# Streaming encoder layer: the prompt's down-projection as seven 2x2 block products, the samples' down-projection beside the up-projection

## The chip, the cores and the metric

The kernel runs on one core of a Trainium2 chip. The metric is the device time in microseconds (us) of one execution. Times are compared as medians of several executions on the same chip; a profiled execution is a further one, of which the hardware profiler recorded every instruction of the five engines (PE, the matrix engine; DVE, the vector engine; ACT, the scalar engine; POOL, the GpSimd engine; SP, which issues the DMAs) and every DMA.

## The reference

One layer of a streaming encoder, for 1024 prompt rows and 8 x 16 = 128 sample rows that share all weights, in float32. The first half (attention, spatial gating, output projection) is not touched by the change. The second half is this:

```python
def conv_ffn(h, conv_cache, w_ffn_in, ffn_conv_w, ffn_conv_b, w_ffn_out):
    g, u = jnp.split(h @ w_ffn_in, 2, axis=-1)          # 1024 -> 2 x 2816
    gp = jnp.concatenate([conv_cache, g], axis=1)
    gc = ffn_conv_b
    for j in range(3):
        gc = gc + ffn_conv_w[j] * gp[:, j:j + T]
    out = (jax.nn.gelu(gc) * u) @ w_ffn_out             # 2816 -> 1024
    return out, gp[:, -2:]
...
x = x + gt2 * conv_ffn(h2, ...)
```

The product with `w_ffn_in` is called the up-projection here, the one with `w_ffn_out` the down-projection. 2816 features are NF = 22 blocks of 128; 1152 rows are 9 tiles of 128 (tile 8 holds the samples).

## The kernel before

**Precision.** Every float32 operand of a matmul is split into a high and a low part (`split`, L77 and L78: ACT copies the high part out, DVE subtracts it from the source), and each product of two operands is three matmuls: high x high, high x low, low x high.

**Up-projection (`unit`, `plain_unit`, `up_weights`).** The kernel already computes it by Winograd's form of Strassen's method: an output of 2x2 blocks from seven block products instead of eight, with sums and differences of blocks on both sides. The operand sums S1 to S4 of the activations stay in SBUF for the whole stage; those of the weights (T1 to T4) are made for every block f of 128 features: four loads into a ring of five staging buffers, four differences on POOL (L1090, L1091, L1095, L1099), seven splits into a ring of nine weight buffers (`wp`). Each f has two units (u = 0, 1; 288 columns of rows each, twice), each of seven products of 12 matmuls 128x288. Unit f = 0, u = 1 is a plain one of eight products. The results go through the convolution (`conv`), GELU and the gate product (`gated`, L1260), and the gated rows are written to DRAM tile by tile (`aT_d[f]`, L1261).

**Order of the work.** Up to the end of f = 0 the order on PE, ACT and DVE is written out by hand (`by_hand`): generators such as `between` (operands of unit pair 0, made during the output projection), `block_pair_1` (operands of unit pair 1, made during f = 0) and `up_weights` are stepped at chosen places of the loops, and an instruction waits behind what stands ahead of it on its engine. From f = 1 on a planner places each instruction by a simulated time: on an engine it takes the ready instruction that is earliest in the program, so instructions whose data and buffers are ready can move ahead. Each engine still runs its own list in order.

**Down-projection (`down_steps`).** It runs at the end. Three groups of three row tiles; in each group, for f = 0..21, a block of `aT_d[f]` (384 rows) and two halves of a row block of `w_ffn_out` are loaded and split, and 3 tiles x 2 halves x 3 matmuls 128x512 are added into six PSUM banks (L1356). The last two f of a group are done tile by tile (`manual_schedule` for PE), and each finished bank is multiplied by the gate (L1389), added to the residual row (L1390) and stored (L1391). The first matmuls of group 0 are stepped during the last unit of the up-projection. `gate_rows` (L824 to L828) issues one load for the prompt's gate and eight for the samples', for each half.

PSUM has six banks of the tag "mm" (X, Y, Z of two units; later the six accumulators) and two of the tag "tp" (transposes). SBUF pools that matter: `xp` (six tiles, operands of the up-projection), `slot` (14 buffers), `wp` (9), `wst` (5 staging buffers).

## Time and profile before

| | |
|---|---|
| median of 3 runs | 1684.75 us (1682.96 to 1686.4) |
| profiled execution, its own time | 1687.31 us |
| its span, first to last instruction | 1685.6 us |
| mean granted TensorE clock | 0.991 |
| up-projection | about 901 to 1417 us of the span |
| down-projection, alone on PE | 1418.6 to 1681 us |

The page gives the busy time of each engine, then the span in 40 slices, the chain of work that ended last, and the costliest groups of instructions. A group's row reads: line, engine, operation, output<-inputs, shape, count | busy time and mean duration of one | idle time of the engine just before them and what ended it. Matmuls overlap each other, so the busy time of a group divided by its count is the pace, and the mean duration is longer than the pace.

### The profile page before, as it was taken

How to read it: one execution, taken by the hardware profiler on the slowest of the kernel's cores; microseconds unless marked ns; L12 is line 12 of the kernel's file. 1: busy time of each engine (PE TensorE's matmuls, PEld its weight loads, DVE VectorE, ACT ScalarE, POOL GpSimd, SP SyncE). 2: the span in 40 equal slices, each digit the busy share in tenths (PEclk: the TensorE clock that was granted, in tenths of full speed). 3: DMA queues.
4: the chain of work that ended last, by engine and by line, in shares of the span. 5: the costliest groups of instructions: out<-in, count | busy, mean ns of one | idle time of the engine just before them, and what ended most of it. 6: DMA issues, size and time to landing. Idle time of an engine off the chain costs nothing.

```text
span 1685.6 us, 28830 instructions
## 1 busy us (share of the span) xinstructions
PE 1642.5 (97%) x10800; PEld 1496.2 (89%) x10800; DVE 926.0 (55%) x1996; ACT 726.0 (43%) x1579; POOL 325.8 (19%) x497
## 2 busy tenths in 40 slices
PE   6999999999999999999997999999999999999998
PEld 4799888799998989999876999999999999888887
DVE  4552111127656643556467877767666675464544
ACT  5443111126655543554245544544444445444342
POOL 5510000015324310024211322222222220000000
PEclk9999999999999999999998999999999999999999
DMA  9215444531110033274532222222222225575765
GB/s 351 72 59 165 150 128 135 175 91 34 50 30 25 22 108 101 88 233 146 178 108 69 84 79 77 68 78 67 70 76 79 80 78 167 181 249 185 229 197 163
DMA packets 166225, 199.15 MB, mean 118 GB/s; under 512 B 14152, under 2 KB 124980, under 8 KB 166085
## 3 DMA queue, kind: packets, MB, share of 16 engines
q1 hardware_dynamic: 166085, 197.31, 36.8%
q8 instruction: 85, 1.39, 0.4%
q14 instruction: 55, 0.45, 0.1%
HBM read 161.74 MB, written 37.57 MB: 118 GB/s over the span
## 4 chain that ended last, share of the span: by engine, by line
PE 90%; DVE 4%; ACT 2%; DMA 2%; issue 1%; SPq 0%; POOL 0%; DVEq 0%; ACTq 0%; POOLq 0%
PE X L1221 16%; PE fops L1356 16%; PE Z L1221 8%; PE Y L1221 4%; PE mxps L1176 4%; PE o L688 2%; PE gbps L103 2%; PE qkps L101 2%; PE gbps L101 2%; PE gbps L102 2%; PE qkps L103 2%; PE qkps L102 2%; PE gaps L101 2%; PE gaps L102 2%; PE gaps L103 2%; PE adaps L382 2%
## 5 line engine op out<-in xcount | busy, mean ns | idle before, releaser
L1356 PE MATMUL fops<-wfo,a 128*128 128x512 f32 x1188 | 270.5, 389 | 0.0
L1356 PEld LDWEIGHTS fops<-wfo,a 128*128 128x128 f32 x1188 | 222.7, 188 | 46.0
L1221 PE MATMUL X<-op,wT 128*128 128x288 f32 x1200 | 190.2, 297 | 6.9 <-ACT u L1283 5.9
L1221 PEld LDWEIGHTS X<-op,wT 128*128 128x128 f32 x1200 | 171.2, 189 | 8.3 <-ACT u L1283 6.4
L1176 PE MATMUL mxps<-wo,mT 128*128 128x512 f32 x432 | 104.6, 397 | 0.5 <-DVE wo L78 0.5
L1176 PEld LDWEIGHTS mxps<-wo,mT 128*128 128x128 f32 x432 | 79.9, 189 | 17.7 <-DVE wo L78 1.1
L1254 DVE SCALAR_TENSOR_TENSOR gc<-gp,parT,gc 128x288 f32<-128x288 f32 (+2 forms) x110 | 65.3, 608 | 42.2 <-ACT gc L1253 42.1
L101 PE MATMUL qkps<-wqk,h1T 128*128 128x256 f32 x288 | 83.5, 290 | 1.0 <-ACT qf L582 1.0
L102 PE MATMUL qkps<-wqk,h1T 128*128 128x256 f32 x288 | 81.9, 284 | 0.0
L103 PE MATMUL qkps<-wqk,h1T 128*128 128x256 f32 x288 | 81.8, 284 | 0.0
L1221 PE MATMUL Z<-opS1h,wT 128*128 128x288 f32 x344 | 76.0, 295 | 0.0
L1253 ACT ACTIVATE gc<-gp,parT 128x288 f32<-128x288 f32 (+2 forms) x110 | 58.9, 573 | 35.3 <-DVE gp L1240 28.8
L1090 POOL TENSOR_TENSOR t<-b,b 128x512 f32<-128x512 f32 x22 | 29.1, 1321 | 224.5 <-DVE wB L78 172.9
L1256 ACT ACTIVATE gc<-gc 128x288 f32<-128x288 f32 x88 | 39.0, 443 | 70.7 <-DVE gc L1255 70.7
L101 PE MATMUL gaps<-h1T,wga 128*128 128x384 f32 x192 | 66.5, 346 | 0.0
L103 PE MATMUL gbps<-h1T,wgb 128*128 128x384 f32 x192 | 65.9, 343 | 0.0
L102 PE MATMUL gaps<-h1T,wga 128*128 128x384 f32 x192 | 65.0, 339 | 0.0
L101 PE MATMUL gbps<-h1T,wgb 128*128 128x384 f32 x192 | 64.9, 338 | 0.0
L102 PE MATMUL gbps<-h1T,wgb 128*128 128x384 f32 x192 | 64.7, 337 | 0.0
L78 DVE TENSOR_TENSOR wB<-b,wB 128x512 fp32r<-128x512 f32 x66 | 57.5, 874 | 12.5 <-ACT wB L77 11.3
L103 PE MATMUL gaps<-h1T,wga 128*128 128x384 f32 x192 | 64.2, 338 | 0.0
L1291 DVE TENSOR_TENSOR upb<-Z,u 128x288 f32<-128x288 f32 x43 | 19.6, 455 | 75.6 <-ACT u L1289 75.6
(497 smaller groups left out, 4339.5 us busy)
## 6 DMA issues: line engine op xcount, KB each, us to landing
adaw<-in_w_ada_dram SPq DMA_DIRECT2D x48, 512.0 KB, 6.5
b<-in_w_ffn_in_dram SPq DMA_DIRECT2D x88, 256.0 KB, 3.1
wfo_0s<-in_w_ffn_out_dram SPq DMA_DIRECT2D x66, 256.0 KB, 3.0
wfo_1s<-in_w_ffn_out_dram SPq DMA_DIRECT2D x66, 256.0 KB, 2.6
aT_d<-gc SPq DMA_DIRECT2D x88, 144.0 KB, 1.8
mb_d<-sgb SPq DMA_DIRECT2D x8, 576.0 KB, 2.7
ga_d<-ga SPq DMA_DIRECT2D x24, 192.0 KB, 1.8
sga<-ga_d SPq DMA_DIRECT2D x8, 576.0 KB, 4.3
```

What stands on the lines that cost most here:

```text
L78: (eng or dve).tensor_tensor(lo, src, hi.bitcast(F32), ALU.subtract)
L101: pe.matmul(ps, lhsT=ah, rhs=bh, start=(i == 0), stop=False)
L102: pe.matmul(ps, lhsT=ah, rhs=bl, start=False, stop=False)
L103: pe.matmul(ps, lhsT=al, rhs=bh, start=False, stop=(i == n - 1))
L382: pe.matmul(ps[32 * j:32 * j + 32, :], lhsT=cT[:, k, :], rhs=st[j // 2][:, (j % 2) * 512:(j % 2 + 1) * 512], start=(k == 0), stop=(k == KD ...
L688: pe.matmul(o[hs, :], lhsT=v[:, k0 // P + i, hs], rhs=out[t, x][:, i * P:(i + 1) * P], start=(i == 0), stop=(i == nk - 1))
L1176: pe.matmul(ps, lhsT=a[:, k, o:o + P], rhs=w[:, b, :], start=(k == n == 0), stop=(k == KD - 1 and n == 2))
L1221: pe.matmul(ps, lhsT=w[:, wj, ks], rhs=x, start=(begin and n == 0), stop=(n == 11), skip_group_check=True)
L1253: act.activation(g, a0, AF.Identity, bias=bb, scale=w0)
L1254: dve.scalar_tensor_tensor(g, a1, w1, g, ALU.mult, ALU.add)
L1256: act.activation(gc, gc, AF.Gelu_apprx_tanh)
L1356: pe.matmul(acc[t, hf], lhsT=a[:, x, o], rhs=w[hf][:, y, :], start=(f == 0 and i == 0), stop=(f == NF - 1 and i == 2))
```

## The change

The down-projection of the eight prompt tiles becomes a 2x2 block scheme: rows 0 to 511 and 512 to 1023, features 0 to 1407 and 1408 to 2815 (NK = 11 blocks each), output columns 0 to 511 and 512 to 1023. Seven products (`KINDS`), each over 11 blocks k and four row tiles at once, three matmuls 128x512 each, replace eight; four PSUM banks X and four Z take the sums. The activation blocks lie whole in SBUF (in the six `xp` tiles and in slots) and S1 to S4 are formed there, S1 on POOL, S2, S3, S4 on DVE, each in place of a block no longer needed. Of the weight sums, T1 is formed in the up-projection and parked in DRAM (`t1_d`), T2 is formed in product S2xT2 and parked (`t2_d`), T3 and T4 are formed in their products, all on POOL with a second operand loaded through three buffers. `prepare` is called three steps ahead of `multiply`; the last four steps are done tile by tile.

The samples' tile leaves the down stage: `gated` splits its 128 columns into `asT[f]`, and `sample_down(f - 1, half)` is called in block f, unit 0, at i = 2 and 3. It loads and splits a half of a row block of `w_ffn_out` (staging and weight rings are shared with `up_weights`) and adds three matmuls into one of the two "tp" banks, which are held until `samples_out`.

In the part ordered by hand, `between` takes its last three splits under the condition that row tile 5 is scaled instead of finished; `block_pair_1` loses one empty step and is stepped once instead of twice at the start; the weights of f = 0 are stepped one place earlier; of the weights of f = 1, four are made in f = 0 (at i = 1, 5, 6, 7) and three in f = 1. The down stage no longer starts inside the last unit, and its loads of gates and cached rows come after its first steps.

```diff
--- before.py
+++ after.py
@@ -135,7 +135,10 @@
     mb_d = dram.tile([KD, P, TOK], F32, name="mb_d")
     ga_d = dram.tile([KD, P, TOK], F32, name="ga_d")
     x1_d = dram.tile([TOK, D], F32, name="x1_d")
-    aT_d = [dram.tile([P, TOK], F32, name=f"aT_d{f}") for f in range(NF)]
+    aT_d = [dram.tile([P, SEQ], F32, name=f"aT_d{f}") for f in range(NF)]
+    NK = NF // 2
+    t1_d = [dram.tile([P, 512], F32, name=f"t1_d{k}") for k in range(NK)]
+    t2_d = [dram.tile([P, 512], F32, name=f"t2_d{k}") for k in range(NK)]
     rel_d = dram.tile([H, 512], F32, name="rel_d")
     relx_d = dram.tile([H, P, 512], F32, name="relx_d")
 
@@ -993,7 +996,7 @@
         o.chunks(1, ("S3h", "S3l", "A22l", "S4h", "S4l"))
         for n in ("S3", "A22", "S4"):
             o.split(n, HOME[n])
-            yield 5, False, 1.3, 1.4
+            yield 5, True, 1.3, 1.4
 
     def block_pair_1():
 
@@ -1033,7 +1036,6 @@
         yield
         o.slots(["S1h"])
         low_slot(o, "S1")
-        yield
         yield
         yield
         o.g["S3h"], o.g["S3l"] = o.g["A21h"], o.g["A21l"]
@@ -1204,7 +1206,8 @@
         step_n += 1
         do_later()
     g1pool.close()
-    fp = ctx.enter_context(tc.tile_pool(name="fp", bufs=1))
+    ffn = ctx.enter_context(ExitStack())
+    fp = ffn.enter_context(tc.tile_pool(name="fp", bufs=1))
 
     def vtile(name, n=QB):
         return fp.tile([P, NV], F32, tag="v", name=name, bufs=16)[:, :n]
@@ -1258,7 +1261,28 @@
 
     def gated(f, c, gc, up):
         dve.tensor_tensor(gc, gc, up, ALU.mult)
-        sp.dma_start(aT_d[f][:, c * QB:(c + 1) * QB], gc)
+        if c == 0:
+            asT[f] = fp.tile([P, 2, P], F32R, tag="as", name=f"as{f}", bufs=2)
+            split(asT[f][:, 0, :], asT[f][:, 1, :], gc[:, :P])
+            gc = gc[:, P:]
+        sp.dma_start(aT_d[f][:, max(c * QB - P, 0):(c + 1) * QB - P], gc)
+    asT, acc_s, raw_s = {}, [], {}
+    def sample_down(f, hf):
+        if f == 0:
+            acc_s.append(tpps(f"sm{hf}"))
+        st = staged(f"ws{f}_{hf}")
+        sp.dma_start(st, wfo[f * P:(f + 1) * P, hf * 512:(hf + 1) * 512])
+        w = wp.tile([P, 2, 512], F32R, tag="w", name=f"wsm{f}_{hf}")
+        split(w[:, 0, :], w[:, 1, :], st)
+        raw_s[hf] = st
+        for i, (x, y) in enumerate(((0, 0), (0, 1), (1, 0))):
+            pe.matmul(acc_s[hf], lhsT=asT[f][:, x, :], rhs=w[:, y, :], start=(f == 0 and i == 0), stop=(f == NF - 1 and i == 2), skip_group_check=True)
+        if hf and f < NK:
+            pool.tensor_tensor(st, st, raw_s[0], ALU.subtract)
+            sp.dma_start(t1_d[f], st)
 
     def unit(f, u, W):
 
@@ -1337,59 +1361,161 @@
             sp.dma_start(cs_[i * P - n0:i * P - n0 + n, :], glo[0:n, i, :])
 
 
-    def down_steps():
...
+    KINDS = [("A11", "B11"), ("A12", "B21"), ("S2", "T2"), ("S1", "T1"), ("S3", "T3"), ("A22", "T4"), ("S4", "B22")]
+    def down():
+        dn = ctx.enter_context(tc.tile_pool(name="dn", bufs=1))
+        g2p, g2s = (dn.tile([P, D], F32, name=n) for n in ("g2p", "g2s"))
+        xs = [xp.tile([P, 3, SEQ], F32, tag=f"x{a}{c}", name=f"ar{c}{a}") for c in range(NC) for a in range(2)]
+        rows = [xs[f // 3][:, f % 3, :] if f < 18 else stile(SEQ, f"ar{f}") for f in range(NF)]
+        s1 = [stile(SEQ, f"ar_s{i}") for i in range((NK + 1) // 2)]
+        kept = {n: [stile(SEQ, f"{n}{i}") for i in range(2)] for n in ("c", "u")}
+        def keep(n, i):
+            return kept[n][i // 2][:, 512 * (i % 2):512 * (i % 2 + 1)]
+        def block(n, k):
+            if n == "S1":
+                return s1[k // 2][:, 512 * (k % 2):512 * (k % 2 + 1)]
+            return rows[k + (NK if n[1] == "2" else 0)][:, 512 * (n[0] == "2"):512 * (n[0] == "2") + 512]
+        def load_a(n, k):
+            f = k + (NK if n[1] == "2" else 0)
+            c = 512 * (n[0] == "2")
+            sp.dma_start(block(n, k), aT_d[f][:, c:c + 512])
+        HOMES = {"A11": "11", "A12": "12", "A22": "22", "S1": "S1", "S2": "11", "S3": "21", "S4": "12"}
+        ops, X, Z = {}, [], []
+        def weight_rows(n, k):
+            f = k + (NK if n[0] == "2" else 0)
+            c = 512 * (n[1] == "2")
+            return wfo[f * P:(f + 1) * P, c:c + 512]
+        def get(src, nm, second=False):
+            t = dn.tile([P, 512], F32, tag="sub", name=nm, bufs=3) if second else staged(nm)
+            sp.dma_start(t, src)
+            return t
+        def prepare(j, k):
+            A, B = KINDS[j]
+            if j == 0:
+                load_a("11", k)
+                load_a("12", k)
+            if j == 1:
+                load_a("21", k)
+                load_a("22", k)
+            if B[0] == "B":
+                t = get(weight_rows(B[1:], k), f"d{B}_{k}")
+            elif B == "T1":
+                t = get(t1_d[k], f"d{B}_{k}")
+            else:
+                x, y = {"T2": (weight_rows("22", k), t1_d[k]), "T3": (weight_rows("22", k), weight_rows("12", k)), "T4": (weight_rows("21", k), t2_d[k])}[B]
+                t, t2 = get(x, f"d{B}_{k}"), get(y, f"d{B}y_{k}", True)
+                pool.tensor_tensor(t, t, t2, ALU.subtract)
+                if B == "T2":
+                    sp.dma_start(t2_d[k], t)
+            w = wp.tile([P, 2, 512], F32R, tag="w", name=f"dw{j}_{k}")
+            split(w[:, 0, :], w[:, 1, :], t)
+            b11, b12, b21, b22, bs1 = (block(n, k) for n in ("11", "12", "21", "22", "S1"))
+            if j == 1:
+                pool.tensor_tensor(bs1, b21, b22, ALU.add)
+            if A == "S2":
+                dve.tensor_tensor(b11, bs1, b11, ALU.subtract)
+            if A == "S3":
+                dve.tensor_tensor(b21, b22, b11, ALU.subtract)
+            if A == "S4":
+                dve.tensor_tensor(b12, b12, b11, ALU.subtract)
+            a = wp.tile([P, 2, 512], F32R, tag="w", name=f"da{j}_{k}")
+            split(a[:, 0, :], a[:, 1, :], block(HOMES[A], k))
+            ops[j, k] = a, w
+        def x1_rows(t, hf):
+            r = dn.tile([P, 512], F32, tag="x1r", name=f"x1r{t}_{hf}", bufs=3)
+            sp.dma_start(r, x1_d[t * P:(t + 1) * P, 512 * hf:512 * (hf + 1)])
+            return r
+        def y_rows(t):
+            return io["o_yp"].rearrange("b s d -> (b s) d")[t * P:(t + 1) * P, :] if t < NTP else io["o_ys"].rearrange("b s d -> (b s) d")
+        def finish(j, i):
+            lo, hi = slice(0, 512), slice(512, 1024)
+            c, u = keep("c", i), keep("u", i)
+            if j == 0:
+                act.activation(c, X[i], AF.Copy)
+            if j == 1:
+                r = x1_rows(i, 0)
+                dve.tensor_tensor(c, Z[i], c, ALU.add)
+                dve.tensor_tensor(c, c, g2p[:, lo], ALU.mult)
+                pool.tensor_tensor(c, c, r, ALU.add)
+                sp.dma_start(y_rows(i)[:, lo], c)
+            if j == 2:
+                r = x1_rows(i, 1)
+                act.activation(u, X[i], AF.Copy)
+                pool.tensor_tensor(u, u, g2p[:, hi], ALU.mult)
+                pool.tensor_tensor(u, u, r, ALU.add)
+            if j == 4:
+                r = x1_rows(i + 4, 1)
+                act.activation(c, X[i], AF.Copy)
+                dve.tensor_tensor(c, Z[i], c, ALU.add)
+                dve.tensor_tensor(c, c, g2p[:, hi], ALU.mult)
+                pool.tensor_tensor(c, c, r, ALU.add)
+                sp.dma_start(y_rows(i + 4)[:, hi], c)
+            if j == 5:
+                r = x1_rows(i + 4, 0)
+                dve.tensor_tensor(c, X[i], g2p[:, lo], ALU.mult)
+                dve.tensor_tensor(c, c, r, ALU.add)
+                sp.dma_start(y_rows(i + 4)[:, lo], c)
+            if j == 6:
+                n = 2 if i == 3 else 1
+                for p in range(n):
+                    a, b = 512 * p // n, 512 * (p + 1) // n
+                    dve.tensor_tensor(c[:, a:b], Z[i][:, a:b], g2p[:, 512 + a:512 + b], ALU.mult)
+                    dve.tensor_tensor(c[:, a:b], c[:, a:b], u[:, a:b], ALU.add)
+                    sp.dma_start(y_rows(i)[:, 512 + a:512 + b], c[:, a:b])
+        def multiply(j, k, i):
+            a, w = ops[j, k]
+            ps = (X if j in (0, 2, 4, 5) else Z)[i]
+            o = slice(i * P, (i + 1) * P)
+            for n, (x, y) in enumerate(((0, 0), (0, 1), (1, 0))):
+                pe.matmul(ps, lhsT=a[:, x, o], rhs=w[:, y, :], start=(j in (0, 1, 3) and k == n == 0), stop=(k == NK - 1 and n == 2), skip_group_check=True)
+            if k == NK - 1:
+                finish(j, i)
+        def samples_out():
+            for j in range(2):
+                gate_rows(2, 2 + j, g2p[:, 512 * j:512 * (j + 1)], g2s[:, 512 * j:512 * (j + 1)])
+            for hf in range(2):
+                cs = slice(512 * hf, 512 * (hf + 1))
+                r, y = x1_rows(NTP, hf), keep("u", hf)
+                dve.tensor_tensor(y, acc_s[hf], g2s[:, cs], ALU.mult)
+                dve.tensor_tensor(y, y, r, ALU.add)
+                sp.dma_start(y_rows(NTP)[:, cs], y)
+        steps = [(j, k) for j in range(len(KINDS)) for k in range(NK)]
+        AHEAD, TAIL = 3, 4
+        for e in steps[:AHEAD]:
+            prepare(*e)
+        X += [mmps(f"dX{i}") for i in range(4)]
+        for n, (j, k) in enumerate(steps[:-TAIL]):
+            if n + AHEAD < len(steps):
+                prepare(*steps[n + AHEAD])
+            if (j, k) == (1, 0):
+                Z += [mmps(f"dZ{i}") for i in range(2)] + [tpps(f"dZ{i}") for i in range(2, 4)]
+            for i in range(4):
+                multiply(j, k, i)
+            if n == 1:
+                samples_out()
+            if n == 3:
+                conv_rows()
+        prepare(*steps[-1])
+        with tc.manual_schedule(engines={pe.engine}):
+            for i in range(4):
+                for e in steps[-TAIL:]:
+                    multiply(*e, i)
 
     prev = None
     for f in range(NF):
@@ -1405,25 +1531,25 @@
                     next(pair1)
                     if (u, i) == (0, 0):
                         later.pop()[1]()
-                        next(pair1)
-                    if u == 0 and i:
+                    if u == 0:
                         next(ws[0], None)
-                if u == 1 and i > 0 if f == 0 else u == 1 or i >= 3:
+                if f == 1 and u == 0 and i < 3:
+                    next(ws[1], None)
+                if f and u == 0 and i in (2, 3):
+                    sample_down(f - 1, i - 2)
+                if (u == 1 and i in (1, 5, 6, 7)) if f == 0 else u == 1 or i >= 3:
                     next(nxt, None)
-                if (f, u) == (NF - 1, 1) and i >= 2:
-                    next(down)
             prev = None if plain else g
         if f == 0:
             for _ in pair1:
                 pass
             by_hand.close()
-        if f == NF - 2:
-            down = down_steps()
-    for _ in range(2):
-        next(prev)
-        next(down)
-    for _ in down:
+    for _ in prev:
         pass
+    for hf in range(2):
+        sample_down(NF - 1, hf)
+    ffn.close()
+    down()
 
 
 _INS = ["x_prompt", "x_sample", "cache_attn_k", "cache_attn_v", "cache_ffn_conv", "c_prompt", "c_sample",
```

47 lines of the change are left out of this document (removed).

## The prediction

> **What bounds the kernel now.** I read the page's engine rows and slices first, then PE by stage, then the waits of PE, then the lists of DVE, POOL and SP where the change adds work.
>
> ```profile
> span 1685.6 us, 28830 instructions
> ...
> PE 1642.5 (97%) x10800; PEld 1496.2 (89%) x10800; DVE 926.0 (55%) x1996; ACT 726.0 (43%) x1579; POOL 325.8 (19%) x497
> ...
> DMA  9215444531110033274532222222222225575765
> GB/s 351 72 59 165 150 128 135 175 91 34 50 30 25 22 108 101 88 233 146 178 108 69 84 79 77 68 78 67 70 76 79 80 78 167 181 249 185 229 197 163
> ```
>
> PE is busy for 97% of the span, so work taken off PE should shorten it, unless something else becomes late. By stage (columns: window, its length, then busy time and instructions of PE, weight loads, DVE, ACT, POOL, then clock, DMA share, GB/s; the windows are the opening of the up-projection, its steady part, the down-projection):
>
> ```profile
> 875.00:960.00 85.00, 71.30 (x445) 64.86 (x445) 65.03 (x99) 46.36 (x87) 23.24 (x28) 0.94 0.23 74
> 1000.00:1380.00 380.00, 380.00 (x2856) 380.00 (x2855) 270.08 (x528) 183.96 (x409) 105.55 (x136) 1.00 0.25 75
> 1420.00:1670.00 250.00, 250.00 (x1105) 206.98 (x1104) 130.72 (x213) 105.55 (x187) 0.00 (x0) 1.00 0.65 207
> ```
>
> In both long stages PE never stops. Only the opening has idle PE: 85.0 - 71.3 = 13.7 us.
>
> **The products taken away.** The down-projection's pace is in the chain of work that ended last (start, length, what, count):
>
> ```profile
> 1418.61 255.75 PE fops L1356 x1128
> ```
>
> 255.75 / 1128 = 0.2267 us a matmul. Before there are 9 tiles x 2 halves x 22 blocks x 3 = 1188. After: 7 x 11 x 4 x 3 = 924 for the prompt (1056 before), and 22 x 2 x 3 = 132 for the samples, as before. The difference is 132 x 0.2267 = **29.9 us**. The samples' matmuls have the same shape wherever they run, so moving 126 of them up (six run after the last block) moves 28.6 us from one stage to the other and saves nothing itself.
>
> **The samples beside the up-projection.** A block f takes 22.37 us now (the same POOL difference at 1101.04 and 1123.41 in the rows below); it becomes 22.37 + 6 x 0.2267 = 23.73. Each block adds two splits of 128x512, a small one, two loads and, for f < 11, one POOL difference and one store. A split costs this:
>
> ```profile
> L77 ACT ACTIVATE wfo<-wfo_0s 128x512 fp32r<-128x512 f32 x66 | 41.7, 631 | 13.4 <-PE fops L1356 8.2 <-DMA wfo_0s<-in_w_ffn_out_dram 4.9
> L78 DVE TENSOR_TENSOR wfo<-wfo_0s,wfo 128x512 fp32r<-128x512 f32 x66 | 45.7, 692 | 17.0 <-ACT wfo L77 16.6 <-DMA wfo_1s<-in_w_ffn_out_dram 0.3
> ```
>
> DVE is busy 270.1 / 380 = 71% there, 15.9 us a block; with 2 x 0.69 + 0.3 (128 columns, an estimate from 0.69 for 512) it has 17.6 of 23.73 (74%), ACT 12.3 (52%). DMA stands at 0.25. PE hides all of it: **0**, with an upper end from the ring of weight buffers. A block now takes 7 + 2 = 9 buffers of the 9, so every refill gets the buffer of its own predecessor, which unit 1 releases; six products (6 x 12 x 0.133 us, 380/2856, = 9.6 us) lie between that and the next use, against 0.63 + 0.69 us of splitting. The staging ring (eight tiles a block in five buffers) closes tighter too: the samples' second tile is followed by a store, a load and three POOL differences before T2 can be split, about 1.8 + 3.1 + 3 x 1.3 = 8.8 us by these medians to landing, of a block's 23.7:
>
> ```profile
> b<-in_w_ffn_in_dram SPq DMA_DIRECT2D x88, 256.0 KB, 3.1
> ...
> aT_d<-gc SPq DMA_DIRECT2D x88, 144.0 KB, 1.8
> ```
>
> **The handover.** Before, the last unit's waits for PSUM copies were filled with the first down matmuls:
>
> ```profile
> 1397.96 0.87 PE L1356 MATMUL fops<-wfo,a 128*128 128x512 f32 x3
> ...
> 1402.11 1.86 PE L1221 MATMUL X<-op,wT 128*128 128x288 f32 x12
> ...
> 1405.41 0.40 PE L1356 MATMUL fops<-wfo,a 128*128 128x512 f32 x1
> ...
> 1407.24 3.38 PE L1356 MATMUL fops<-wfo,a 128*128 128x512 f32 x14
> ...
> 1412.06 1.53 PE L1356 MATMUL fops<-wfo,a 128*128 128x512 f32 x6
> ```
>
> That is 24 matmuls, 5.4 us. After, six of samples (1.4 us) can stand there for certain; the rest only if the first block step has its operands, whose `xp` tile comes free when unit 0 has finished A22 (the row at 1402.11), 8 us before the last of these gaps. So it costs between 0 and 4.1 us. SP also gets 18 gate loads while the first steps run:
>
> ```profile
> L828 SPq DMA_DIRECT2D g2s<-ada_d x16: 318/418/1137, 1388.4 to 1397.9; - x16
> ```
>
> 18 x 0.418 = 7.5 us of SP, in whose queue the loads of step 5 and later stand behind; they have three steps' lead, 3 x 12 x 0.2267 = 8.2 us. Between 0 and 2 us. I take **+2** for both, because the planner already moved loads ahead of their place (in these rows, the gates among them).
>
> **DVE and POOL in the seven products.** A step is 12 matmuls, 2.72 us of PE. DVE has two splits (1.38 us) in every step, a third 128x512 operation in S2, S3 and S4 (2.07 us); POOL has one difference in the steps of A12, S2, S3 and A22. Either engine alone fits under 2.72. Together they may not:
>
> ```profile
> 1100.27 0.69 DVE L78 TENSOR_TENSOR wB<-b,wB 128x512 fp32r<-128x512 f32 x1
> 1101.57 1.31 DVE L78 TENSOR_TENSOR wB<-b,wB 128x512 fp32r<-128x512 f32 x1 [0.61 <-ACT wB L77]
> ...
> 1102.95 1.15 DVE L1243 COPY glast<-gp 128x2 f32<-128x2 f32 x1
> ```
>
> ```profile
> 1101.04 1.29 POOL L1090 TENSOR_TENSOR t<-b,b 128x512 f32<-128x512 f32 x1 [8.96 <-DVE wB L78]
> 1102.41 1.63 POOL L1091 TENSOR_TENSOR b<-b,b 128x512 f32<-128x512 f32 x1
> ...
> 1123.41 1.29 POOL L1090 TENSOR_TENSOR t<-b,b 128x512 f32<-128x512 f32 x1 [8.96 <-DVE wB L78]
> ```
>
> The split that met the POOL difference ended 0.55 us after it, and took 1.31 instead of 0.69; the two run one after the other. The Trainium skill ("SBUF — State Buffer", section "SBUF: two separate sides") says so: a DVE operation with two SBUF inputs and a GpSimd operation that reads SBUF take turns on an exclusive lock. By that rule the trace agrees, and engine shares taken one by one mislead here. So S2 and S3 steps need 3 x 0.69 + 1.29 = 3.36 us of the pair, A12 and A22 steps 2.67. Worst case, nothing made earlier than three steps ahead: in S2 the last eight steps need 8 x 3.36 = 26.9, and the four results of A12 (gate on DVE, residual on POOL) 4 x (0.69 + 1.29) = 7.9, together 34.8 us where PE gives 10 x 2.72 = 27.2: 7.6 late. From S3 to A22 likewise: S3's lead shrinks to 0.3 us, then 7.9 + 11 x 2.67 = 37.3 against 29.9 + 0.3: 7.1 late. Worst 14.7 us. Best 0: in the first product the pair needs only 1.38 of 2.72, and POOL's S1 sums and DVE's S2 sums are free to be made in that time, as their blocks stay in place. I take **+3**, nearer to the cover.
>
> **DMA in the first three products.** Each step of them moves 3 x 256 KB; 33 steps 26.0 MB, with gates, residuals and results 28.7 MB in 33 x 2.72 = 89.8 us, 320 GB/s. The page's best slice holds 351 at a share of 0.9, the best of the down stage 249 at 0.7. Operand tiles come free in the last unit already and later products need less, so I take 0; price in the rivals.
>
> **The opening.** PE's waits from 875 to 960:
>
> ```profile
> PE X L1221 <- ACT u L1283: 5.9, 1, 5.9
> PE h2ps L935 <- ACT raw L921: 3.0, 1, 3.0
> PE h2ps L935 <- DVE x L1147: 2.2, 1, 2.2
> ```
>
> The 5.9 us: PE waits for the copy u2 (L1283), which stands on ACT behind eight modulations, A11's split, four modulations and A12's split:
>
> ```profile
> 906.00 2.90 ACT L921 ACTIVATE raw<-h2psT,S,G 128x128 f32<-128x128 f32 x8 [2.18 <-PE h2psT L960]
> 908.75 1.20 ACT L914 ACTIVATE opA11h<-raw 128x1152 fp32r<-128x1152 f32 x1
> ...
> 914.07 0.44 ACT L921 ACTIVATE raw<-h2psT,S,G 128x128 f32<-128x128 f32 x1
> ...
> 916.64 1.15 ACT L914 ACTIVATE opA12h<-raw 128x1152 fp32r<-128x1152 f32 x1
> ...
> 918.21 0.40 ACT L1283 ACTIVATE u<-X 128x288 f32<-128x288 f32 x1
> ```
>
> With `block_pair_1` stepped once less there, the last five go behind u2 (918.21 - 914.07 = 4.1 us earlier, less a weight's split that comes there instead), but then u3, which A22 waits for, stands behind them: most of the wait reappears one product later. The later splits of A22 and S4 let tile 5's scaling pass, which ends the 2.2 us. Against it, three weights of f = 1 are made after the plain unit's last convolution; each a product too late would cost 3 x 1.6 = 4.8 us. DVE has 65.0 of 85 us, so little more than the waits is to be had. From -11.1 (all three gone) to +5; I take **-2**.
>
> **The sum.** -29.9 + 0 + 2 + 3 - 2 = -26.9 on the profiled execution's 1687.31, which is 1660.4. That execution is 2.56 above the median of the runs, so 1684.75 - 26.9 = 1657.9: **1658 us**. The tail stays: one bank's gate, sum and store after PE's last matmul.
>
> **Rivals.**
> - *The pair DVE and POOL decides in S2 and A22.* For it: the lock in the rows above; against: the free time in the first product. 11 (the middle of the upper half of 0 to 14.7) in place of 3: 1666.
> - *DMA decides in the first three products.* If it keeps no more than the down stage's best slice, 249 GB/s, they take 28.7 MB / 249 = 115.3 us, less 89.8 and 8.2 of lead: +17.3. 1658 - 3 + 17.3 = 1672. Against it: the 351. The skill's table in the same page ("A bandwidth-pool intuition that's wrong") puts HBM at about 358 GB/s a core; no stall would follow by that figure.
> - *The opening is cleared* and the pair costs nothing: 1684.75 - 29.9 + 2 - 11.1 = 1646.
> - *The full ring makes it slower.* A refill of a weight buffer stands on ACT ahead of the PSUM copy that PE needs, and waits for unit 1's release; ACT runs in order, so PE waits for ACT and ACT for PE's next product. One product, 1.6 us, lost in each of 21 blocks is 33.6: 1691. It decides against the gain from 26.9 / 21 = 1.3 us a block. For it, this row of ACT's waits from 960 to 1390 (us in total, times, longest); against it, 0.4 us each, and PE did not stop:
>
> ```profile
> ACT wB L77 <- PE X L1221: 6.6, 18, 0.4
> ```
>
> That the samples don't ride along but pile up at the end would leave the sum of matmuls as it is.
>
> **How the numbers follow.** Forecast 0.58, with its own range 1650 to 1664 (lock at 0 and opening 5 us better, or both 3 us worse); pair 0.20; DMA 0.06; cleared opening 0.10; slower 0.06. Range 1645 to 1675: the forecast, the pair, the DMA case and most of the cleared opening; the slower case is left out. A measurement of this kernel tells about 0.2% (3.4 us) from no change. Faster by more than that: 0.92; within: 0.02; slower: 0.06.
>
> **What would show it.** After: 924 + 132 matmuls 128x512 at 0.227 us, blocks of 23.7 us with PE at 100%, a stage of seven products of 209.5 us plus its stalls. The lock shows as DVE splits above 1 us and PE waiting for DVE in S2 and A22; DMA as PE or ACT waiting for loads at shares near 1; the ring as PE waiting for ACT in every block. A block longer than 24.5 us, or the seven products above 225 us, makes the forecast wrong.

## The result, and the profile after

The changed kernel takes 1695.8 us (median of 4 runs, 1694.2 to 1697.4) against 1685.6 us for the kernel before beside it: ratio 1.0063, 95% interval 1.0048 to 1.0078. Forecast were 1658 us and a range of 1645 to 1675, so the change is slower where it was said to be faster. Its profiled execution took 1697.21 us. Of all the runs below, two single executions are slow ones (2631 us in ord_dve_open, 3179 us in t_early2) and are left out of the medians and ratios given here.

The page of the changed kernel: span, the busy rows of PE, DVE and POOL, and the slices of DMA and throughput.

```profile
span 1695.3 us, 28634 instructions
...
PE 1623.9 (96%) x10668; PEld 1477.3 (87%) x10668; DVE 983.6 (58%) x2051; ACT 738.5 (44%) x1613; POOL 456.0 (27%) x568
...
DMA  9214434531110133274531233333323233857562
GB/s 352 68 57 163 152 126 135 175 91 34 50 29 25 24 105 112 87 236 139 175 107 65 83 101 94 110 97 106 95 81 97 86 92 116 286 205 250 191 206 98
```

PE issues 132 instructions fewer, as worked out, and is busy 18.6 us less; yet the span is 9.7 us longer. The same windows of the changed kernel as before, then four of its down stage (window, length, busy time and instructions of PE, weight loads, DVE, ACT, POOL, then clock, DMA share, GB/s):

```profile
875.00:960.00 85.00, 70.22 (x396) 62.96 (x395) 66.77 (x101) 46.09 (x86) 19.33 (x23) 0.88 0.25 81
1000.00:1380.00 380.00, 380.00 (x2781) 375.59 (x2781) 263.05 (x543) 194.72 (x432) 112.79 (x137) 1.00 0.31 95
```

```profile
1450.00:1480.00 30.00, 17.97 (x89) 14.84 (x87) 10.53 (x18) 4.02 (x8) 8.77 (x7) 0.84 0.78 272
1480.00:1500.00 20.00, 13.25 (x50) 10.84 (x51) 13.79 (x23) 8.68 (x16) 8.50 (x1) 0.73 0.99 350
1500.00:1550.00 50.00, 45.14 (x186) 35.25 (x186) 44.69 (x60) 19.13 (x35) 33.51 (x13) 0.97 0.43 144
1550.00:1600.00 50.00, 48.07 (x208) 38.75 (x209) 42.32 (x41) 22.64 (x40) 32.47 (x21) 1.00 0.72 238
```

The steady up-projection is as forecast: PE never stops, with the samples' matmuls in it. In the four windows of the down stage it is idle for 12.0, 6.8, 4.9 and 1.9 us, and in the first two at a lower clock; in the opening the clock is 0.88 instead of 0.94. PE's waits of the changed kernel follow (us in total, times, longest). There da and dw are the split blocks of activations and weights of the seven products, dX and dZ their sums in PSUM, glt and glo the transposed cached rows; wB is a weight of the up-projection, raw its scaled rows, u a copy from its PSUM banks.

```profile
PE dX L1484 <- ACT da L77: 11.7, 1, 11.7
PE glt L1351 <- DVE u L1494: 7.1, 1, 7.1
PE dX L1484 <- DVE da L78: 5.6, 6, 3.1
PE h2ps L938 <- ACT raw L924: 5.1, 2, 4.8
PE Y L1224 <- ACT wB L77: 3.9, 1, 3.9
PE X L1224 <- ACT u L1307: 2.5, 1, 2.5
PE X L1224 <- ACT u L1313: 1.7, 1, 1.7
```

Three of them are in the down stage. Its PE list (start, length, what, count, in brackets the idle time before):

```profile
1453.04 13.81 PE L1484 MATMUL dX<-dw,da 128*128 128x512 f32 x60
1473.96 1.12 PE L1351 MATMUL glt<-ident,glast 128*128 128x128 f32 x4 [7.11 <-DVE u L1494]
1486.75 5.52 PE L1484 MATMUL dX<-dw,da 128*128 128x512 f32 x15 [11.67 <-ACT da L77]
```

Of 924 matmuls 24 ran before 1453.04 as filler, and the last ends near 1691. The other 900 need 900 x 0.2267 = 204 us and took 238: **34 us** are lost, 20 of them between 1466.9 and 1486.75. What the stop of 11.7 us hung on is in ACT's and SP's lists:

```profile
1485.55 0.63 ACT L77 ACTIVATE dw<-dB 128x512 fp32r<-128x512 f32 x1 [27.98 <-DMA dB<-in_w_ffn_out_dram]
```

```profile
1463.24 0.32 SPq L1386 DMA_DIRECT2D ar<-aT_d  x1
1467.39 0.32 SPq L829 DMA_DIRECT2D g2p<-ada_d  x1
1467.75 3.67 SPq L831 DMA_DIRECT2D g2s<-ada_d  x8
...
1476.64 0.33 SPq L1357 DMA_DIRECT2D o_cp_dram<-glo  x1
...
1481.13 0.45 SPq L1398 DMA_DIRECT2D dB<-in_w_ffn_out_dram  x1
```

No weight of the first product is loaded between these rows. The chain is read from these rows and the code; the first run below tests its link through `glo`, the other links are not tested alone: `conv_rows` takes its tile `glo` from the five staging buffers (`staged`, L1352), which are handed out in the order of the program, so the eighth weight is given none ahead of `glo`, and SP's list has its load behind `glo`'s stores. `glo` is copied from transposes `glt` (L1351), which need one of the two "tp" banks; both are held by the samples' sums until `samples_out` has multiplied them by the gates; and the gates' pool takes the memory of the up-projection's small tiles, which come free with the last store of gated rows. So every step of the down stage behind the seventh hung on the end of the up-projection.

### The profile page after: what moved, and what is told of

It reads as the page before. It is cut to its first block, busy times and chain, and to the rows that moved or that the text cites. A ratio compares the mean times of both kernels' runs of the same rounds, so it can differ in the third digit from the quotient of the medians.

```text
span 1695.3 us, 28634 instructions
## 1 busy us (share of the span) xinstructions
PE 1623.9 (96%) x10668; PEld 1477.3 (87%) x10668; DVE 983.6 (58%) x2051; ACT 738.5 (44%) x1613; POOL 456.0 (27%) x568
## 4 chain that ended last, share of the span: by engine, by line
PE 82%; DVE 6%; DMA 4%; POOL 2%; ACT 2%; issue 2%; SPq 1%; DVEq 0%; ACTq 0%; POOLq 0%
PE X L1224 16%; PE Z L1224 8%; PE Y L1224 4%; PE mxps L1178 4%; PE dZ L1484 4%; PE dX L1484 3%; PE o L691 2%; PE qkps L101 2%; PE qkps L103 2%; PE qkps L102 2%; PE gaps L101 2%; PE gaps L102 2%; PE gbps L103 2%; PE gaps L103 2%; PE adaps L385 2%; PE gbps L101 2%
## 5 line engine op out<-in xcount | busy, mean ns | idle before, releaser
L1484 PE MATMUL dX<-dw,da 128*128 128x512 f32 x528 | 127.1, 399 | 18.0 <-ACT da L77 11.7
L1484 PEld LDWEIGHTS dX<-dw,da 128*128 128x128 f32 x528 | 100.7, 192 | 42.8 <-ACT da L77 12.1
L1484 PE MATMUL dZ<-dw,da 128*128 128x512 f32 x396 | 91.2, 390 | 0.6 <-DVE da L78 0.5
L1484 PEld LDWEIGHTS dZ<-dw,da 128*128 128x128 f32 x396 | 74.2, 188 | 16.8 <-DVE da L78 1.0
L1257 DVE SCALAR_TENSOR_TENSOR gc<-gp,parT,gc 128x288 f32<-128x288 f32 (+2 forms) x110 | 64.2, 598 | 15.9 <-ACT gc L1256 15.9
L1258 DVE SCALAR_TENSOR_TENSOR gc<-gp,parT,gc 128x288 f32<-128x288 f32 (+2 forms) x110 | 70.9, 660 | 0.1
L77 ACT ACTIVATE da<-ar 128x512 fp32r<-128x512 f32 x66 | 41.5, 629 | 67.2 <-PE dX L1484 36.9
L78 DVE TENSOR_TENSOR da<-ar,da 128x512 fp32r<-128x512 f32 x66 | 57.3, 868 | 22.8 <-ACT da L77 22.7
L101 PE MATMUL gaps<-h1T,wga 128*128 128x384 f32 x192 | 66.4, 346 | 0.0
L103 PE MATMUL gbps<-h1T,wgb 128*128 128x384 f32 x192 | 65.9, 343 | 0.0
L78 DVE TENSOR_TENSOR wT<-t,wT 128x512 fp32r<-128x512 f32 x44 | 43.7, 994 | 36.9 <-ACT wT L77 36.4
L102 PE MATMUL gaps<-h1T,wga 128*128 128x384 f32 x192 | 65.0, 339 | 0.0
L101 PE MATMUL gbps<-h1T,wgb 128*128 128x384 f32 x192 | 64.9, 338 | 0.0
```

Source lines behind the costliest of these rows:

```text
L77: act.activation(hi, src, AF.Copy)
L78: (eng or dve).tensor_tensor(lo, src, hi.bitcast(F32), ALU.subtract)
L101: pe.matmul(ps, lhsT=ah, rhs=bh, start=(i == 0), stop=False)
L102: pe.matmul(ps, lhsT=ah, rhs=bl, start=False, stop=False)
L103: pe.matmul(ps, lhsT=al, rhs=bh, start=False, stop=(i == n - 1))
L1257: dve.scalar_tensor_tensor(g, a1, w1, g, ALU.mult, ALU.add)
```

## The experiments

All are compared with the kernel before, run beside them on the same chip (1684.9 to 1685.6 us). Five chips were used, so runs from different chips are compared by their ratios to it. Lines left out of an edit are marked by three dots.

### The stop at the handover

**glo_own**: the changed kernel, `glo` taken out of the staging ring, into the three buffers of the second operands.

```diff
-        glo = staged("glo").rearrange("p (i n) -> p i n", i=4)
+        glo = fin.tile([P, 512], F32, tag="sub", name="glo", bufs=3).rearrange("p (i n) -> p i n", i=4)
...
```

> Only the buffer of the transposed cached rows (glo) changes: it comes from the three buffers of the second operands instead of the ring of five staging buffers. Theory A (buffer order): the load of step 7's weights gets its staging buffer only after glo, and glo is written only after transposes that wait for a PSUM bank that the samples hold until their gates have landed; freed of that, the 11.7 us in which PE waits for step 7 go, and perhaps the 7.1 us of the transposes: 1676 to 1684 us. Theory B (the queue): the 18 gate loads and the early row loads on SP hold back step 7; they stay where they are, so the time stays at 1692 or more.

Measured 1679.6 us, ratio 0.9966 (0.9954 to 0.9978): 16 us less, and faster than before. The stops of 11.7 and 7.1 us are gone. One buffer was 16 of the 20 us lost at the handover. PE's waits left in its down stage:

```profile
PE dZ L1486 <- DVE da L78: 8.3, 6, 3.6
PE dX L1486 <- DVE da L78: 3.1, 4, 1.2
PE dZ L1486 <- DVE glo L1353: 0.5, 1, 0.5
```

**late_only**: glo_own, with the samples' end and the gate rows later.

```diff
-            if n == 1:
+            if n == 7:
                 samples_out()
-            if n == 3:
+            if n == 9:
                 conv_rows()
```

> The changed kernel with the rows of the short output taken from the small ring (as in glo_own, 1679.6 us), and besides with the samples' end put behind the eighth step of the first product and the gate rows behind the tenth, so that the 18 gate loads stand on SP behind more loads of the first product. VectorE's order is still the planner's. Theory A (what is left is VectorE's order: sums for products 3 to 5 stand ahead of the next splits): 1677 to 1681, TensorE still waits some 10 us for da and dw in products 2 and 3. Theory B (the lock between VectorE and GpSimd): the same, 1677 to 1681. Theory C (the gate loads on SP make the loads of product 2 late): 1670 to 1674, the stop of 3.6 us near 1486 us gone.

1676.6 us, 0.9947 (0.9931 to 0.9964). That is 3 us under glo_own with overlapping intervals, in the gap between the two expected spans. It is the base of the runs below.

### The opening

**open_back**: the changed kernel with the opening's order of before.

```diff
-            yield 5, True, 1.3, 1.4
+            yield 5, False, 1.3, 1.4
...
-                    if u == 0:
+                        next(pair1)
+                    if u == 0 and i:
                         next(ws[0], None)
-                if f == 1 and u == 0 and i < 3:
-                    next(ws[1], None)
...
-                if (u == 1 and i in (1, 5, 6, 7)) if f == 0 else u == 1 or i >= 3:
+                if u == 1 and i > 0 if f == 0 else u == 1 or i >= 3:
```

> The changes to the hand-written order of the opening (between, block_pair_1, the places where the weights of f = 0 and f = 1 are stepped) are undone, everything else stays. Theory A: the later weights of f = 1 cost the opening about 5 us (PE waits 3.9 us for B21 and runs at a lower clock after it): 1690 to 1692 us. Theory B: the loss comes from the samples' weights entering the rings in f = 1, whatever the order of the opening: 1694 to 1697.

1690.8 us, 1.0035 (1.0023 to 1.0048): 5 us less. The new order costs what the forecast had as its upper end, where it took a gain of 2.

**open_w**: the changed kernel with only the last two edits of open_back, the weights of block 1.

> The changed kernel (1695.8 us) with only the order of the second block's weights put back (all seven made during the plain unit), the rest of the opening's order (when the sums of pair 1 are split, when the first weights and the scaling of pair 1 come) left as changed. Theory A (the 3.9 us wait for the weight B21 of block 1, and the clock after it, is what the opening lost): 1690 to 1692, as open_back (1690.8). Theory H (the earlier steps moved a wait for the operands of pair 1 and its split work, and the weights only take their place): 1694 to 1697, another wait in its place.

1694.0 us, 1.0048 (1.0033 to 1.0064): between the two, told apart from neither. The traces say more. From the same transposes near 889 us to the same matmul of the samples near 1400 us, the rows of the changed kernel, of open_w and of open_back (in this order):

```profile
891.25 0.38 PE L938 MATMUL h2ps<-ident,x 128*128 128x128 f32 x2
1406.60 0.87 PE L1282 MATMUL sm<-wsm,as 128*128 128x512 f32 x3
```

```profile
887.64 0.38 PE L938 MATMUL h2ps<-ident,x 128*128 128x128 f32 x2
1400.01 0.87 PE L1282 MATMUL sm<-wsm,as 128*128 128x512 f32 x3
```

```profile
887.84 0.38 PE L938 MATMUL h2ps<-ident,x 128*128 128x128 f32 x2
1398.13 0.87 PE L1283 MATMUL sm<-wsm,as 128*128 128x512 f32 x3
```

515.35, 512.37 and 510.29 us: the weights are 3.0 of the 5.1 us, by one profile each. In open_w the wait for wB of 3.9 us is gone; its down stage waits longer (14.2 us for da on ACT instead of 11.7), which gives part of it back, and why is open. So the weights are not shown to be worth their 3.0 us in the kernel's time.

### VectorE and GpSimd in products 2 to 5

**dve_diffs**: the changed kernel with its differences and S1 sums on VectorE.

```diff
-                pool.tensor_tensor(t, t, t2, ALU.subtract)
+                dve.tensor_tensor(t, t, t2, ALU.subtract)
...
-                pool.tensor_tensor(bs1, b21, b22, ALU.add)
+                dve.tensor_tensor(bs1, b21, b22, ALU.add)
```

> The weight differences T2, T3, T4 and the row sums S1 of the down stage are made by DVE instead of POOL, everything else stays. Theory A (lock): POOL and DVE shut each other out, so DVE alone is quicker (0.6 us an operation instead of 1.3 of the pair), and PE's waits for DVE in the second and third products, some 6 us with a lower clock after them, go: 1684 to 1690 us. Theory B: DVE is late there because the loads are late after the handover: 1693 to 1698, DVE's load being higher now.

1695.1 us, 1.0056 (1.0037 to 1.0076): no change that can be told. The stops of the handover are as they were (11.1 and 7.3 us), PE's waits for da fell from 5.6 to 1.7 us, and waits for dw grew from 0.6 to 5.2. **all3** adds to it the opening of open_back, the samples' end at step 6 and the gate rows at step 8 (with `glo` still in the staging ring):

> The opening's order undone, the differences and sums on DVE, and the samples' result and the cached rows moved behind steps 6 and 8 instead of 1 and 3. Theory A (three separate losses of about 5, 10 and 20 us): 1657 to 1666 us. Theory B (a common cause, DMA or DVE too slow for the seven products): 1672 or more, with PE still waiting in the first three products.

1687.5 us, 1.0008 (0.9994 to 1.0021). The gains don't add up: PE still waits for ACT's and DVE's parts of the operands (5.5, 4.3, 2.7, 2.6 us). Work moved off GpSimd onto VectorE fills VectorE, so these two runs can't tell its load from the turns that the two engines take. I then suspected VectorE's order: in glo_own the planner puts sums for products 3 to 5 ahead of splits that PE waits for.

**ord_dve**: late_only with VectorE in the order of the program in the down stage.

```diff
...
+        in_order.enter_context(tc.manual_schedule(engines={dve.engine}))
...
```

> late_only, with VectorE's instructions of the down stage in the order of the program, three steps ahead of TensorE, in place of the planner's. Theory A (VectorE's order): the sums no longer stand ahead of splits that TensorE waits for; the 11.6 us of waits for da and dw in glo_own fall to 2 or less, the time to 1668 (1664 to 1672). Theory B (the lock makes the operations themselves long): the operations keep their 1.3 to 1.8 us beside GpSimd, the waits stay, 1676 to 1682. Theory C (loads): as late_only within 2 us.

**ord_nolock**: ord_dve plus the edits of dve_diffs. **ord_dve_open**: ord_dve plus those of open_back.

> ord_dve, with the 33 differences and the 11 sums S1 on VectorE instead of GpSimd (44 operations of 0.68 us more on VectorE, some 30 us over the stage, and no GpSimd operation beside it but the ends' adds). Theory A (order): the waits were gone already, so the same as ord_dve within 2 us. Theory B (lock): the splits run at 0.68 us, the waits fall, 1666 to 1670, some 10 us under ord_dve. Theory C: as ord_dve.

> ord_dve, with the opening's order of before put back (the edits of open_back). The opening cost 5 us by open_back against the changed kernel, and nothing of the later stages hangs on it: 5 us under ord_dve, 1663 if theory A holds (1659 to 1668), 1672 if it doesn't. If the two losses cover each other, as in all3, it comes out within 2 us of ord_dve.

ord_dve took 1695.4 us (1.0052, 1.0033 to 1.0072), ord_nolock 1714.0 (1.0168, 1.0151 to 1.0186) and ord_dve_open 1689.6 (1.0020, 1.0004 to 1.0035). The theory of the order fell: the program's order is 19 us worse than the planner's. DVE's list of ord_dve shows why: a chain of split, sum, ACT and split with 0.78 us of standing still in every step of the third product, and 12.8 us for gates and rows:

```profile
1474.53 0.69 DVE L1496 TENSOR_TENSOR u<-sm,g2s 128x512 f32<-128x512 f32 x1 [8.19 <-DMA g2s<-ada_d]
1479.80 0.69 DVE L1497 TENSOR_TENSOR u<-u,x1r 128x512 f32<-128x512 f32 x1 [4.58 <-DMA x1r<-x_d]
...
1531.21 1.77 DVE L78 TENSOR_TENSOR dw<-dT,dw 128x512 fp32r<-128x512 f32 x1
1532.90 1.77 DVE L1427 TENSOR_TENSOR ar<-ar_s,ar 128x512 f32<-128x512 f32 x1
1535.45 0.69 DVE L78 TENSOR_TENSOR da<-ar,da 128x512 fp32r<-128x512 f32 x1 [0.78 <-ACT da L77]
```

The opening's 5 us came again (1695.4 to 1689.6, with intervals that just overlap), so that loss adds to the others. ord_nolock, 19 us above ord_dve, again says only that VectorE has no room for 44 more operations here.

**ord_ahead**: ord_dve with S2, S3 and S4 written one product earlier and the gates loaded three steps ahead.

```diff
-            if A == "S3":
-                dve.tensor_tensor(b21, b22, b11, ALU.subtract)
...
             ops[j, k] = a, w
+            if j == 2:
...
+                dve.tensor_tensor(b21, b22, b11, ALU.subtract)
```

> ord_dve (1695.4 us), still with VectorE in the order of the program, but the sums S2, S3 and S4 are written one product ahead of the splits that use them, and the samples' gates are loaded three steps ahead of their use. In ord_dve each step of the third product was a chain of sum on VectorE, copy on ScalarE and split on VectorE with 0.78 us of standing still in it, and VectorE stood 12.8 us for gates and rows. Theory E (the program's order was slow for these two reasons; what the planner did well was to put the sums ahead): both gone, 1672 to 1680, no worse than late_only by more than 3 us. Theory F (VectorE has too much to do in products 2 and 3 in any order, beside a GpSimd that takes turns with it): 1685 or more.

1681.0 us, 0.9970 (0.9955 to 0.9985): 14 us of ord_dve's 19 are these two reasons, a little beyond the span expected; the planner's order of late_only still measured 4 us less, with intervals that overlap. No order tried here was better than the planner's.

**t_early**: late_only with the differences T2, T3, T4 made in the up-projection.

```diff
+        if hf and f >= NK:
+            k = f - NK
+            t = fp.tile([P, 512], F32, tag="td", name=f"td{f}", bufs=1)
+            sp.dma_start(t, t1_d[k])
+            pool.tensor_tensor(t, st, t, ALU.subtract)
+            sp.dma_start(t2_d[k], t)
...
-                pool.tensor_tensor(t, t, t2, ALU.subtract)
...
+                t = get({"T1": t1_d, "T2": t2_d, "T3": t3_d, "T4": t4_d}[B][k], f"d{B}_{k}")
```

> late_only (1676.6 us), with the 33 differences of the down-projection's weights made on GpSimd during the up-projection, beside the samples' weights, stored to DRAM and loaded once in the down stage: 33 operations of GpSimd, 33 loads and 11 stores leave the down stage; the up-projection gets 2 loads, 3 stores and 3 operations of GpSimd more in each of its last 11 blocks (and 14 buffers instead of 16 for its small tiles). Nothing is added to VectorE. Theory B (what is left in products 2 and 3 is the lock between VectorE and GpSimd): the 4.5 us of waits for da and dw in the third product go, 1670 to 1673. Theory D (VectorE stands still for dependences at the edges of the products, whatever GpSimd does): 1675 to 1678. If the up-projection's ring of 5 weight buffers can't bear it, its block of 23.7 us grows, and the time by 11 times that.

1671.6 us, 0.9917 (0.9900 to 0.9933): 5 us less than late_only, with intervals that touch, as the theory of the turns had it. The group of weight splits of VectorE from 1455 to 1645 us, in late_only and in t_early (busy, mean ns):

```profile
L78 DVE TENSOR_TENSOR dw<-dT,dw 128x512 fp32r<-128x512 f32 x44 | 45.5, 1034 | 2.0 <-ACT dw L77 1.9
```

```profile
L78 DVE TENSOR_TENSOR dw<-dT,dw 128x512 fp32r<-128x512 f32 x44 | 35.6, 810 | 5.7 <-ACT dw L77 5.7
```

But 44 transfers left the down stage with the 33 operations. **t_loads** puts the transfers back without the operations, **t_ops** the operations without the transfers:

```diff
+                if B != "T1":
+                    get({"T2": t1_d[k], "T3": weight_rows("12", k), "T4": t2_d[k]}[B], f"d{B}y_{k}", True)
+                if B == "T2":
+                    sp.dma_start(t5_d[k], t)
```

```diff
+                if B != "T1":
+                    x = dn.tile([P, 512], F32, tag="sub", name=f"idle{B}_{k}", bufs=3)
+                    pool.tensor_tensor(x, t, t, ALU.subtract)
```

> t_early (1671.6 us) with the transfers of the down stage as before: the 33 second operands are loaded again (and not used) and the 11 stores of T2 are made again, to a place that nobody reads; only GpSimd's 33 differences stay out of the down stage. Theory B (what t_early gained, 5.0 us against late_only, is GpSimd's operations, which take turns with VectorE's): within 1.5 us of t_early, 1670 to 1673. Theory G (it is the DMAs and SP's queue of which t_early took 44 out): back to late_only, 1675 to 1678.

> t_early once more, as the measure for t_ops on the same chip and beside the same runs of the kernel before: 1670 to 1673.

> t_early with 33 operations of GpSimd of the size of the differences put back into the down stage, each behind the load of its product's weight, with an output that nobody reads; no transfer is added and nothing waits for them. Theory B (GpSimd's operations slow VectorE's by taking turns with them): the splits beside them take 1.8 us instead of 0.7 again and TensorE waits for da and dw in the third product; 1674 to 1677. Theory G (transfers and SP's queue, since t_loads came out between the two): as t_early2 within 1.5 us. Theory I (not the turns, but that the splits wait for the differences): as t_early2 too, but with the long operations.

t_loads: 1673.2 us, 0.9939 (0.9918 to 0.9959). t_early2, the same kernel as t_early: 1671.9, 0.9922 (0.9907 to 0.9938). t_ops: 1679.3, 0.9962 (0.9949 to 0.9976). The transfers cost nothing that can be told from t_early2. The idle operations cost 7.4 us by these medians and 6.7 by the ratios, with intervals apart: more than expected, though nobody waits for their results. Nor do loads wait for them to let go of a staging buffer: in SP's list of t_ops those waits are for VectorE's splits, none for GpSimd. PE's waits of t_ops and the same group of splits, in t_early 810 ns each:

```profile
PE dZ L1495 <- DVE da L78: 4.4, 3, 2.8
PE dX L1495 <- ACT da L77: 4.2, 1, 4.2
PE dX L1495 <- DVE da L78: 2.7, 2, 2.4
```

```profile
L78 DVE TENSOR_TENSOR dw<-dT,dw 128x512 fp32r<-128x512 f32 x44 | 39.6, 901 | 1.1 <-ACT dw L77 1.1
```

So GpSimd's operations cost by taking turns with VectorE's, at about 6.7 / 33 = 0.2 us each. The splits became longer than in t_early by 4.0 us in this group alone, and PE's waits for DVE's da are 7.1 us, against 2.5 in t_early2 (the wait for ACT's da lies at the handover and is in both, 4.2 and 5.2 us).

### A version that beats both

**t_early_open** is t_early with open_back's edits, **ahead_te_open** is ord_ahead with both, and **t_last_open** is t_early_open with the last pair of blocks (k = 10) left in the down stage:

```diff
-        if hf and f >= NK:
+        if hf and NK <= f < NF - 1:
...
```

> t_early with the opening's order of before put back: 5 us under t_early, as ord_dve_open lay 5.3 under ord_dve; 1665 to 1668 by theory B, 1670 to 1673 by theory D. The version that should beat both kernels with the planner's order left alone.

> ord_ahead with the differences made in the up-projection as in t_early and with the opening's order of before. Sum of the three if none covers another: opening 5 us, differences 4 to 6 us under ord_ahead, so 1662 to 1670. If theory F holds for ord_ahead, the taking away of the differences gains more here than in t_early, 10 us and more.

> t_early_open (1667.5 us) with the three differences of the last pair of blocks left in the down stage, as in late_only; those of the ten pairs before stay in the up-projection. In t_early_open TensorE stood 4.8 us at 1436 us, where GpSimd's copy of a halo stood behind a difference that waited for its load, and SP behind the same. If that is the cause: 4 to 5 us less, 1662 to 1664. If the stop comes from the row loads of the first product instead, it stays: 1667 within 1.5.

t_early_open: 1667.5 us, 0.9895 (0.9876 to 0.9914), **1.0% faster than before**. ahead_te_open: 1675.2, 0.9935 (0.9920 to 0.9949), outside its span; its samples' end stops PE for 6.2 us. t_last_open: 1667.0, 0.9887 (0.9868 to 0.9906), no different. The explanation by the halo copy fell: GpSimd's copy no longer waits, but the stop stays, 3.5 us instead of 4.8, and ACT's row of t_last_open names the rows of the first product, which SP issues just before:

```profile
1440.68 0.63 ACT L77 ACTIVATE da<-ar 128x512 fp32r<-128x512 f32 x1 [4.31 <-DMA ar<-aT_d]
```

## Why the prediction was wrong

Against the forecast of -26.9 us stand +10.2 us, 37 us apart. The sign that the prediction set for itself came: the 900 matmuls of the seven products behind the filler took 238 us, above its 225. By the trace the handover has 18 of the 37 us (20 lost, 2 forecast) and the products behind it 11 (14 lost, 3 forecast), by open_back the opening has 7 (5 lost, 2 of gain forecast).

- **The products taken away, -29.9:** right. 132 instructions fewer, and where PE isn't stopped it keeps the pace of before, 30.08 / 132 = 0.228 us, here in PE's list of late_only:

```profile
1551.99 30.08 PE L1486 MATMUL dZ<-dw,da 128*128 128x512 f32 x132
```

- **The samples beside the up-projection, 0:** right. A block of the changed kernel took 1125.82 - 1102.09 = 23.73 us, the figure forecast, with PE at 100%. The full ring didn't bind; the rival that put the loss there named the right side for a wrong reason.
- **The handover, +2:** wrong, and the largest miss: some 20 us in the trace, 16 by glo_own. The filler that this step feared for was there (24 matmuls). The failed sentence is that the loads of step 5 and later stand behind 18 gate loads and have 8.2 us of lead. It priced the gate loads' time on SP and not what they wait for, and left `conv_rows` out, whose tile ties the staging ring to the samples' banks and these to the gates. "The planner already moved loads ahead of their place" holds only where a buffer is free, and buffers come in program order.
- **DVE and POOL, +3:** the mechanism was right and the size off. In the changed kernel the stage behind 1487 us lost 34 - 20 = 14 us in all, near the upper end of its range of 0 to 14.7; 33 operations of GpSimd cost 6.7 in t_ops, the low clock behind the stop 1.9 (13.25 us for 50 matmuls that take 11.3), and the rest wasn't taken apart. The free time of the first product, by which I took the value near the cover, wasn't there. In the changed kernel the stop lies in it; and in late_only, without the stop, VectorE is busy for 17.8 of 20 us while the S1 sums are made, with splits of 1.77 us beside them (window, length, busy time of PE, weight loads, DVE, ACT, POOL, clock, DMA share, GB/s):

```profile
1460.00:1480.00 20.00, 19.81 (x90) 16.11 (x88) 17.76 (x15) 8.88 (x16) 14.89 (x9) 1.00 0.78 266
```

- **DMA, 0:** right for the three products as a whole: 33 loads and 11 stores more cost nothing that can be told (t_loads), and the window from 1480 to 1500 us moved 350 GB/s, where the rival on DMA had a bound of 249.
- **The opening, -2:** wrong in sign: +5, its upper end. u2's wait fell from 5.9 to 2.5 and came back in part as u3's 1.7, and the wait for scaled rows went (2.2 to 0.3), as said. But the wait for raw grew from 3.0 to 4.8, and the price that I had named and not taken was due: the weight B21 of block 1 came late (3.9 us), 3.0 us of the stage by the profile of open_w.
- **The chances:** 0.92 for faster rested on PE being the bound in every stage. Only the rival of the full ring, 0.06, stood for a dependence through a ring of buffers, and only in the up-projection; nothing was held for one at the seam of the two stages.

What stays open: why open_w's gain didn't reach the end, and about 9 us between t_early_open and the forecast, of which its trace shows a stop of 4.8 us at the handover and one of 3.2 us for da.

## What to carry to other kernels

When work is moved to the seam of two stages, follow each tile it takes through its pool: what it waits for, and what is handed a buffer of the same ring after it. That was worth 16 us here, and it is seen by reading SP's list for the next load that doesn't come, not by adding up durations. Work of GpSimd that nobody waits for isn't free where VectorE has little time left (busy for 84% of 1440 to 1640 us in late_only): put it in a stage with slack (5 us here) rather than on VectorE (no gain in dve_diffs, 19 us worse in ord_nolock, in the program's order).

## What the runs showed of the hardware

**GpSimd doesn't get its turn.** I had reckoned that an operation of GpSimd waits for one of VectorE. In late_only one sum took 13.81 us, about ten times its usual 1.3, while VectorE ran some twenty operations with two inputs back to back. It ended when VectorE had nothing ready; t_ops and t_early have such a sum of 13.70 and 13.17 us. GpSimd's row of late_only, then VectorE's:

```profile
1486.60 13.81 POOL L1425 TENSOR_TENSOR ar_s<-ar,ar 128x512 f32<-128x512 f32 x1 [11.69 <-issue]
```

```profile
1498.57 0.70 DVE L78 TENSOR_TENSOR dw<-dB,dw 128x512 fp32r<-128x512 f32 x1
1500.45 1.77 DVE L1427 TENSOR_TENSOR ar<-ar_s,ar 128x512 f32<-128x512 f32 x1 [1.18 <-POOL ar_s L1425]
```

The Trainium skill ("SBUF — State Buffer", section "SBUF: two separate sides") has whichever of the two starts first hold the pair of ports "for the whole instruction". The trace agrees for one instruction (VectorE's at 1500.45, beside GpSimd's next one, takes 1.77 us in place of 0.69), and adds that VectorE's next ones come ahead of a GpSimd operation that waits.

**A stop costs more than its length.** After the stop of 3.92 us in the opening the next product took 3.50 us, where this product takes 1.76 us in the steady part; behind the stop of 11.67 us the granted clock of the window was 0.73, and PE needed 13.25 us for 50 matmuls that take 11.3 at 0.2267:

```profile
945.21 3.50 PE L1224 MATMUL Y<-op,wB 128*128 128x288 f32 x12 [3.92 <-ACT wB L77]
...
1419.20 1.76 PE L1224 MATMUL Y<-op,wB 128*128 128x288 f32 x12
```
